# A hybrid attention trunk on one core: the linear attention's products start four projection tiles earlier, and the next norm waits for them as a chain

## The chip, the cores and the metric

The kernel runs on one NeuronCore of a Trainium2 chip. The core has a matrix engine (TensorE, in the profile PE, with its weight loads shown as PEld), three engines for elementwise work (VectorE or DVE, ScalarE or ACT, GpSimd or POOL) and a queue that mostly issues transfers (SyncE or SP). Each engine works off its own queue in order and waits for the others through semaphores. The metric is the device time of one execution in microseconds (us).

## What is computed

One layer of a streaming encoder, on 2048 tokens of width 1024, in float32. One input projection feeds three groups of heads, which all read the same normalised input; the groups are gated, concatenated, and mapped back by one output projection.

```python
h = rmsnorm(x, norm_g)
z = h @ w_in                    # columns: aq ak av ag | mq mk mv mo mi mf mg | gq gk gv ga gg
y_a = band_chunk_attention(aq, ak, av, rel_bias) * silu(ag)
qk  = silu(causal_conv([mq, mk], conv_w))
y_b = sigmoid(mo) * head_rmsnorm(mlstm_chunkwise(qk, mv, mi, mf)) * silu(mg)
log_alpha = log_sigmoid(ga @ w_alpha + b_alpha) / 16
y_c = head_rmsnorm(gla_chunkwise(gq, gk, gv, log_alpha)) * silu(gg)
out = rmsnorm(x + [y_a, y_b, y_c] @ w_out, final_g)
```

The linear attention (GLA) is the part that moves here. Inside a chunk it needs, for every pair of a query and an earlier key, a product over the channels with a decay of its own for each channel. The kernel forms the nearest pairs (within 16 tokens) one distance at a time.

## The kernel before

The first phase goes through four blocks (NQ = 4) of 512 tokens (QT). For each block it runs the projections as tiles of 24 matmuls of 512 columns (three for each of 8 k-tiles, since each operand is split in a high and a low part). A tile is cut in two pieces of 12 matmuls. In program order a block has:

- proj_z (2 tiles: GLA's queries and keys), proj_v (4 tiles for the mLSTM's values, then proj_gg with 2 tiles for GLA's gate, then 4 tiles for the attention's values);
- proj_m (6 tiles, with the convolution on DVE), proj_gm (6 tiles, the mLSTM's gates), proj_a (9 tiles, the attention's queries, keys and gate; in the last block 5, the others follow in the second phase).

The smaller work runs beside the projections as generators, called chains:

- **prep** normalises the next block's x. prep_x (called before proj_m) loads x and takes the mean square; prep itself multiplies a ones matrix by the diagonal of the scales (L299), loads xT (4 DMAs on SP), scales it with eight DVE operations (L308) and projects the gates' inputs (L315). split_x then splits the result in high and low parts (L329, L330).
- **gates** prepares the gates of the mLSTM and of GLA: L337 and L344 on PE, a chain of ACT and DVE operations, four transposes (L379) and six small products (L388); it leaves `ls`, `rt` and `iwl`.
- **gla_in** handles two halves of 256 tokens. For each of 16 distances POOL forms a product (L652) and updates the decayed keys (L649); after each four distances PE sums them over the channels (L658). Each half has four such groups.
- **gla** follows it in four pieces, two per half: PE transposes and scores (L688 to L692), DVE assembles them (L699, L702), PE takes output and state (L709 to L716), and after a norm the output is transposed (L739) and gated (L741).
- **mlstm** goes through four chunks: L531 and a DVE/ACT decay (L534, L536); L541 with L545; L559 to L576; then DVE and POOL normalise (L585 to L601) and PE transposes the result (L610).

PE's order is written by hand in program order, and a small planner named Flow decides where a chain's next step is put. Its clock advances by 12 x 0.227 us at each piece of a projection. A chain yields (PE time, gap): its next step is due when the clock has passed the gap, and it is issued at the first piece after that. `flow.need(name)` issues the due steps of all chains, without any projection between them, until the named chain has ended. The other engines' order comes from a scheduler that takes ready instructions by priority; weight splits and PSUM evacuations have a high priority.

The PSUM bank `pw` exists once. prep, gates and gla_in all use it, and gla_in holds it through a whole half. That is why the old code calls `flow.need("gla_in")` before it starts prep. The names and lines above are those of the kernel before.

The second phase (from about 972 us) holds the banded attention and the output projection; the change does not touch it.

Of the kernel before, what the change touches and what calls it, by code (L numbers as in the profile page):

```python
# [22 lines left out]
NC = QT // L  # L23
# [81 lines left out]
def trunk_kernel(ctx: ExitStack, tc: tile.TileContext, xT, x, w_f, w_t, w_o, w_gates, norm_g, conv_w,  # L105
# [3 lines left out]
    NQ = S // QT  # L109
# [23 lines left out]
    flow = Flow()  # L133
# [8 lines left out]
    with ExitStack() as pa_:  # L142
# [151 lines left out]

        def prep(q, R, dg):
            t0 = q * QT
            yield 0.0, 0.0
            rb = bank("pw")
            nc.tensor.matmul(rb, ones, dg.rearrange("p a t -> p (a t)"), start=True, stop=True)  # L299
            rbs = g_tile([P, QT])  # L300
            nc.scalar.copy(rbs, rb)
            raws = []
            for g in range(4):
                raw = xraws.tile([P, 2, QT], FP32, name="xraw")
                nc.sync.dma_start(raw, xT[:, 2 * g:2 * g + 2, t0:t0 + QT])
                for j in range(2):
                    k = 2 * g + j
                    nc.vector.scalar_tensor_tensor(raw[:, j, :], raw[:, j, :], ng[:, k:k + 1], rbs, op0=ALU.mult, op1=ALU.mult)  # L308
                raws.append(raw)
            yield 0.9, 8.0  # L310
            gp = bank("pw")
            for g in range(4):
                for j in range(2):
                    k = 2 * g + j
                    nc.tensor.matmul(gp[32 * (k % 4):32 * (k % 4) + 32, :], wg[:, k, :], raws[g][:, j, :],  # L315
                                     start=(k < 4), stop=(k >= 4), skip_group_check=True)
                if g % 2 == 1:
                    yield 2.0, 2.0
            g1 = g_tile([P, QT])
            nc.scalar.activation(g1, gp, AF.Identity, bias=onerow)  # L320
            R["raws"], R["g1"] = raws, g1
# [121 lines left out]
        def proj_gg(X):  # L443
            gg = big.tile([P, 2, QT], FP32, name="gg", bufs=1)
            for b in range(2):
                ps = proj_f(f"gg{b}", X)
                th = silu_tile(ps)
                nc.gpsimd.tensor_scalar(gg[:, b, :], th, glg[:, b:b + 1], None, op0=ALU.mult)
            return gg
# [70 lines left out]
        def mlstm(q, qk, vs, R):  # L520
            rt, iwl = R["rt"], R["iwl"]
            for c in range(NC):
# [78 lines left out]
                nc.vector.tensor_tensor(hb.rearrange("p a b d -> p b a d"), ov[:, :, :, 0:64],  # L601
                                        sm[:, 3].unsqueeze(3).broadcast_to([P, 2, 3, 64]), op=ALU.mult)
                hf = hb.rearrange("p a b d -> p (a b d)")
                yield 1.7, 9.0
                while "gm" not in R:
                    yield 0.0, 1.0
                gm = R["gm"]
# [10 lines left out]

        b16 = lambda t: t.rearrange("p (b i) -> p b i", i=16)

        def gla_in(q, z, ls_all, G):
            NB = ST // 16
            for sub in range(2):
                ts_ = slice(sub * ST, (sub + 1) * ST)
                qq, k, ls = z[:, 0, ts_], z[:, 1, ts_], ls_all[:, ts_]
                al = one.tile([P, ST], FP32, name="al")
                nc.scalar.activation(al, ls, AF.Exp, scale=1.0 / 16)
                gk = one.tile([P, ST], FP32, name="gk")
                nc.gpsimd.tensor_copy(gk, k)
                lc = big.tile([P, ST], FP32, name="lc")  # L630
                nc.vector.tensor_tensor_scan(lc, rst16, ls, 0.0, op0=ALU.mult, op1=ALU.add)
                qt = big.tile([P, ST], FP32, name="qt")
                nc.scalar.activation(qt, lc, AF.Exp, scale=1.0 / 16)
                dl = big.tile([P, 2, 8], FP32, name="dl")
                nc.vector.tensor_copy(dl, qt.rearrange("p (c b i) -> p c b i", c=2, i=16)[:, :, :, 15])
                nc.vector.tensor_tensor(b16(lc), b16(lc)[:, :, 15:16].broadcast_to([P, NB, 16]), b16(lc), op=ALU.subtract)
                nc.scalar.activation(lc, lc, AF.Exp, scale=1.0 / 16)
                nc.vector.tensor_tensor(lc, lc, k, op=ALU.mult)
                nc.vector.tensor_tensor(qt, qq, qt, op=ALU.mult)
                Dt = big.tile([P, 2, 9, 9], FP32, name="Dt")  # L640
                nc.gpsimd.memset(Dt, 1.0)
                for i in range(1, 9):
                    nc.vector.tensor_tensor(Dt[:, :, i, 0:i], Dt[:, :, i - 1, 0:i],
                                            dl[:, :, i - 1:i].broadcast_to([P, 2, i]), op=ALU.mult)
                dr_ps = bank("pw")
                yield 0.0, 4.0
                for c in range(16):
                    if c:
                        nc.gpsimd.tensor_tensor(b16(gk)[:, :, 0:c], b16(gk)[:, :, 0:c],  # L649
                                                b16(al)[:, :, c:c + 1].broadcast_to([P, NB, c]), op=ALU.mult)  # L650
                    pc = b16(prd[:, c % NP, :])
                    nc.gpsimd.tensor_tensor(pc[:, :, 0:c + 1], b16(gk)[:, :, 0:c + 1],  # L652
                                            b16(qq)[:, :, c:c + 1].broadcast_to([P, NB, c + 1]), op=ALU.mult)
                    if c % NP == NP - 1:
                        yield 0.0, 6.0
                        for e in range(c - NP + 1, c + 1):
                            w = 16 if e < 4 else e + 1
                            nc.tensor.matmul(b16(dr_ps[32 * (e % 4):32 * (e % 4) + 32, 0:ST])[:, :, 0:w], hs4[:, e // 4, :],  # L658
                                             b16(prd[:, e % NP, :])[:, :, 0:w], start=(e < 4), stop=(e >= 12), skip_group_check=True)
                        yield 0.35, 0.0  # L660
                dr = n_tile([P, ST], "dr")
                nc.scalar.copy(dr, dr_ps[:, 0:ST])
                G[sub] = (lc, qt, Dt, dr)
# [83 lines left out]
        R = {}  # L747
# [3 lines left out]
        X = split_x(R["raws"])  # L751
        flow.start("gates", gates(0, R["g1"], R))
        for q in range(NQ):
            st["q"] = q
            flow.need("gla_in")
            flow.need("gla")
            z = proj_z(X)
            vs, vg, gg = proj_v(X, lambda: proj_gg(X))
            flow.need("gates")
            G = {}  # L760
            flow.start("gla_in", gla_in(q, z, R["ls"], G))
            flow.start("gla", gla(q, vg, gg, G))
            flow.need("mlstm")
            if q + 1 < NQ:
                dg = prep_x(q + 1)
            qk = proj_m(X)
            M = dict(R)
            flow.start("mlstm", mlstm(q, qk, vs, M))
            M["gm"] = proj_gm(X)
            if q + 1 < NQ:  # L770
                flow.need("gla_in")
                R = {}
                flow.start("prep", prep(q + 1, R, dg))
            proj_a(q, X)
            if q + 1 < NQ:
                flow.need("prep")
                X = split_x(R["raws"])
                flow.start("gates", gates(q + 1, R["g1"], R))
# [332 lines left out]
```

## Time and profile before

| | us |
|---|---|
| median of 3 runs | 1402.09 |
| lowest and highest run | 1397.63, 1406.93 |
| the profiled execution | 1396.99 |
| its span, first to last instruction | 1395.3 |
| its mean granted TensorE clock | 0.958 |

A profile is of one execution. "Busy" is the time in which an engine ran instructions; matmuls overlap, so a busy PE need not run at its peak. The granted clock is the share of full speed that TensorE got. In a view of windows each line is a stretch of time with the busy time of each engine in it. In a view of waits each line says which instruction stood idle and which one ended its wait. In a timeline each line has its start and its duration, then the engine, the kernel's line, the operation and the tiles.

### The profile page before, as it was taken

To read this page: it belongs to the slowest core of one execution; us is meant where nothing else is said; L and a number is where in the kernel's file an instruction comes from. 1 tells how busy PE (TensorE), PEld (TensorE's weight loads), DVE (VectorE), ACT (ScalarE), POOL (GpSimd) and SP (SyncE) were. 2 spreads that over 40 slices of the span, in tenths; PEclk is the share of its full clock that TensorE was granted. 3 is DMA by queue.
4 is the path that set the end of the run, shared out by engine and by line. 5 is a ranking of instruction groups with operands and counts; after the bars stand their busy time and mean duration, and the time that the engine had idled before them with its cause. 6 is when DMAs were issued, how large, how long until landed. Compare 5 with 4: busy or idle time off the path is not lost.

```text
span 1395.3 us, 20018 instructions
## 1 busy us (share of the span) xinstructions
PE 1308.3 (94%) x7044; PEld 1060.7 (76%) x7044; DVE 809.1 (58%) x1886; ACT 602.4 (43%) x1149; POOL 609.2 (44%) x847
## 2 busy tenths in 40 slices
PE   4999999999998999999899999997968999999997
PEld 2787778788777878877688787886857877877876
DVE  7626566562856556474556547555657756756731
ACT  5634322563432365343135434221566645645631
POOL 4225752431665234277322526631354453453452
PEclk7999999999998999999899999996969999999999
DMA  7444224534322463422233542231596654554222
GB/s 247 141 134 135 76 71 140 190 114 136 106 77 66 135 236 90 142 87 81 75 106 117 144 151 91 82 110 49 164 274 182 183 157 149 164 170 153 78 76 84
DMA packets 107205, 180.10 MB, mean 129 GB/s; under 512 B 9824, under 2 KB 54752, under 8 KB 107104
## 3 DMA queue, kind: packets, MB, share of 16 engines
q1 hardware_dynamic: 102496, 170.43, 40.2%
q10 hardware_dynamic: 4608, 8.39, 1.6%
q8 instruction: 56, 0.92, 0.3%
q14 instruction: 45, 0.37, 0.1%
HBM read 143.14 MB, written 35.65 MB: 128 GB/s over the span
## 4 chain that ended last, share of the span: by engine, by line
PE 72%; DVE 11%; DMA 5%; ACT 4%; POOL 3%; issue 3%; SPq 1%; POOLq 0%; DVEq 0%; ACTq 0%
PE ip L243 12%; PE ip L245 11%; PE ip L244 11%; PE ip L263 3%; PE ip L265 3%; PE ip L264 3%; PE s L860 3%; PE ip L984 3%; PE ip L982 3%; PE ip L983 3%; PE tp L924 2%; DVE pt L874 2%; PE ga L692 2%; PE w L941 2%; DMA wraw<-in_w_o 2%
## 5 line engine op out<-in xcount | busy, mean ns | idle before, releaser
L243 PE MATMUL ip<-x,w 128*128 128x512 f32 x800 | 329.5, 412 | 0.0
L245 PE MATMUL ip<-x,w 128*128 128x512 f32 x800 | 314.4, 393 | 0.0
L244 PE MATMUL ip<-x,w 128*128 128x512 f32 x800 | 313.8, 392 | 0.0
L243 PEld LDWEIGHTS ip<-x,w 128*128 128x128 f32 x800 | 151.3, 189 | 45.6 <-issue 15.9
L245 PEld LDWEIGHTS ip<-x,w 128*128 128x128 f32 x800 | 151.3, 189 | 33.9
L244 PEld LDWEIGHTS ip<-x,w 128*128 128x128 f32 x800 | 151.8, 190 | 30.0 <-issue 2.6
L236 POOL TENSOR_TENSOR w<-wraw,w 128x1024 fp32r<-128x1024 f32 x44 | 106.2, 2413 | 149.1 <-ACT w L235 149.1
L235 ACT CAST w<-wraw 128x1024 fp32r<-128x1024 f32 x132 | 138.1, 1047 | 60.5 <-DMA wraw<-in_w_t 25.3
L236 DVE TENSOR_TENSOR w<-wraw,w 128x1024 fp32r<-128x1024 f32 x88 | 119.5, 1358 | 76.4 <-ACT w L235 74.9
L879 POOL TENSOR_SCALAR pt<-pt,sm 128x640 f32<-128x640 f32 (+2 forms) x96 | 70.5, 736 | 147.9 <-DVE sm L878 116.9
L982 PE MATMUL ip<-wo,y 128*128 128x512 f32 x256 | 106.7, 417 | 0.0
L263 PE MATMUL ip<-w,x 128*128 128x512 f32 x256 | 100.4, 392 | 3.6 <-ACT vg L426 3.5
L877 ACT ACTIVATE pt<-pt,sm 128x640 f32<-128x640 f32 (+2 forms) x96 | 73.3, 763 | 69.8 <-DVE sm L874 67.4
L984 PE MATMUL ip<-wo,y 128*128 128x512 f32 x256 | 101.4, 396 | 0.3 <-POOL y L890 0.3
L983 PE MATMUL ip<-wo,y 128*128 128x512 f32 x256 | 101.2, 395 | 0.0
L265 PE MATMUL ip<-w,x 128*128 128x512 f32 x256 | 99.7, 389 | 0.0
L264 PE MATMUL ip<-w,x 128*128 128x512 f32 x256 | 99.6, 389 | 0.0
L930 DVE TENSOR_TENSOR pl<-tp,ph 128x512 fp32r<-128x512 f32 (+2 forms) x126 | 74.6, 599 | 32.0 <-ACT ph L929 30.7
L860 PE MATMUL s<-kk,qq 128*128 128x384 f32 (+1 forms) x360 | 80.9, 334 | 12.4 <-DVE sm L874 10.7
L652 POOL TENSOR_TENSOR prd<-gk,zg 128x16 f32<-128x16 f32 (+15 forms) x128 | 72.2, 564 | 31.1 <-PE pw L658 24.5
L860 PEld LDWEIGHTS s<-kk,qq 128*128 128x128 f32 x360 | 60.6, 201 | 31.3 <-DVE sm L874 25.0
L929 ACT CAST ph<-tp 128x512 fp32r<-128x512 f32 (+2 forms) x126 | 63.0, 509 | 34.1 <-PE tp L924 33.3
(244 smaller groups left out, 2413.9 us busy)
## 6 DMA issues: line engine op xcount, KB each, us to landing
wraw<-in_w_f SPq DMA_DIRECT2D x100, 512.0 KB, 3.6
wraw<-in_w_t SPq DMA_DIRECT2D x32, 512.0 KB, 3.7
qq<-q_d SPq DMA_DIRECT2D x48, 256.0 KB, 4.3
kk<-k_d SPq DMA_DIRECT2D x18, 512.0 KB, 6.3
vv<-v_d SPq DMA_DIRECT2D x18, 512.0 KB, 7.1
xraw<-in_x SPq DMA_DIRECT2D x16, 512.0 KB, 5.0
xraw<-in_xT SPq DMA_DIRECT2D x16, 512.0 KB, 6.4
xr<-in_x SPq DMA_DIRECT2D x16, 512.0 KB, 3.7
```

What stands on the lines that cost most here:

```text
L235: nc.scalar.copy(w[:, :, 0, :], rv)
L236: other().tensor_tensor(w[:, :, 1, :], rv, f32(w[:, :, 0, :]), op=ALU.subtract)
L243: nc.tensor.matmul(ps, w[:, k, 0, :], X[k][:, 0, :], start=(k == 0), stop=False)
L244: nc.tensor.matmul(ps, w[:, k, 0, :], X[k][:, 1, :], start=False, stop=False)
L245: nc.tensor.matmul(ps, w[:, k, 1, :], X[k][:, 0, :], start=False, stop=(k == KT - 1))
L263: nc.tensor.matmul(ps, X[k][:, 0, t], w[:, 0, :], start=(k == 0), stop=False)
L264: nc.tensor.matmul(ps, X[k][:, 0, t], w[:, 1, :], start=False, stop=False)
L265: nc.tensor.matmul(ps, X[k][:, 1, t], w[:, 0, :], start=False, stop=(k == KT - 1))
L860: nc.tensor.matmul(sp[:, :cn], qq[:, l, tt * P:(tt + 1) * P], kk[:, ko + c0:ko + c0 + cn], start=(l == 0), stop=(l == 1))
L982: nc.tensor.matmul(ps, Y[k][:, 0, t], wo[k, j][:, 0, :], start=(e == 0), stop=False)
L983: nc.tensor.matmul(ps, Y[k][:, 0, t], wo[k, j][:, 1, :], start=False, stop=False)
L984: nc.tensor.matmul(ps, Y[k][:, 1, t], wo[k, j][:, 0, :], start=False, stop=(e == KT - 1))
```

## The change

gla_in is started inside proj_v, after proj_gg and before the four tiles of the attention's values; it was started after them. It now takes the gates' results from the dictionary R and waits, as a chain, until `iwl` is there. The wait for the gates moves from the end of proj_v to the end of proj_m. `flow.need("gla_in")` before prep is gone: prep, as a chain, yields until gla_in has ended. In all blocks but the last, the mLSTM's last chunk has its final transpose due 17 us after the step before it, where it was 9.

```diff
         def prep(q, R, dg):
             t0 = q * QT
-            yield 0.0, 0.0
+            while "gla_in" in flow.chains:
+                yield 0.0, 1.0
             rb = bank("pw")
...
                 hf = hb.rearrange("p a b d -> p (a b d)")
-                yield 1.7, 9.0
+                yield 1.7, 9.0 if c < NC - 1 or q == NQ - 1 else 17.0
                 while "gm" not in R:
...
-        def gla_in(q, z, ls_all, G):
+        def gla_in(q, z, R, G):
             NB = ST // 16
+            while "iwl" not in R:
+                yield 0.0, 1.0
+            ls_all = R["ls"]
             for sub in range(2):
...
             z = proj_z(X)
-            vs, vg, gg = proj_v(X, lambda: proj_gg(X))
-            flow.need("gates")
             G = {}
-            flow.start("gla_in", gla_in(q, z, R["ls"], G))
+
+            def between():
+                g = proj_gg(X)
+                flow.start("gla_in", gla_in(q, z, R, G))
+                return g
+
+            vs, vg, gg = proj_v(X, between)
             flow.start("gla", gla(q, vg, gg, G))
             flow.need("mlstm")
             if q + 1 < NQ:
                 dg = prep_x(q + 1)
             qk = proj_m(X)
+            flow.need("gates")
             M = dict(R)
             flow.start("mlstm", mlstm(q, qk, vs, M))
             M["gm"] = proj_gm(X)
             if q + 1 < NQ:
-                flow.need("gla_in")
                 R = {}
                 flow.start("prep", prep(q + 1, R, dg))
             proj_a(q, X)
```

## The prediction

> **What bounds the kernel now.** I read the page first. TensorE (PE) is busy 94% of the span and carries 72% of the chain that ended last; in the 40 slices (35 us each) its granted clock dips at the start, to 8 tenths in slices 13 and 20, and to 6 in slices 28 and 30.
>
> ```profile
> PE 1308.3 (94%) x7044; PEld 1060.7 (76%) x7044; DVE 809.1 (58%) x1886; ACT 602.4 (43%) x1149; POOL 609.2 (44%) x847
> PEclk7999999999998999999899999996969999999999
> PE 72%; DVE 11%; DMA 5%; ACT 4%; POOL 3%; issue 3%; SPq 1%; POOLq 0%; DVEq 0%; ACTq 0%
> ```
>
> So time is saved only where PE stands or runs slowly. The change touches the first phase alone (four blocks of 512 tokens, until about 972 us), so I cut windows there: a clean stretch of projections, a clean stretch of mixed work (212.10), the three places where the planner empties the product chain before the next norm (179.92, 417.95, 654.53, the last with its aftermath at 671.01), two turns from one block to the next (270.46, 510.15), and the tail of the phase. Columns: window, its length, busy us of PE, weight loads, DVE, ACT, POOL, then PE's granted clock.
>
> ```profile
> 103.56:119.98 16.42, 16.42 (x74) 13.34 (x72) 9.06 (x10) 7.86 (x12) 5.97 (x5) 1.00 0.58 181
> 179.92:194.09 14.17, 11.45 (x86) 8.85 (x85) 9.56 (x25) 4.21 (x9) 12.82 (x25) 0.76 0.26 75
> 212.10:228.00 15.90, 15.90 (x127) 12.24 (x125) 9.87 (x26) 4.90 (x10) 4.04 (x9) 1.00 0.47 154
> 270.46:277.01 6.55, 4.40 (x19) 2.86 (x18) 2.50 (x4) 3.63 (x8) 4.38 (x4) 1.00 0.88 341
> 417.95:433.78 15.83, 11.93 (x85) 8.71 (x84) 8.79 (x22) 4.21 (x9) 13.47 (x24) 0.68 0.19 54
> 510.15:515.56 5.41, 4.19 (x19) 2.94 (x18) 2.63 (x4) 3.58 (x9) 2.14 (x3) 1.00 0.98 385
> 654.53:671.01 16.48, 11.78 (x86) 8.92 (x85) 9.97 (x26) 4.21 (x9) 13.46 (x25) 0.79 0.20 53
> 671.01:696.06 25.05, 21.36 (x99) 16.91 (x98) 14.54 (x27) 4.45 (x7) 4.89 (x6) 0.86 0.26 85
> 937.16:971.74 34.58, 24.74 (x165) 22.52 (x163) 21.01 (x67) 5.70 (x13) 8.12 (x19) 0.71 0.14 36
> ```
>
> The first window holds 72 projection matmuls: 16.42/6 = 2.74 us for a piece of 12, the planner's unit. In the three barrier windows POOL is busy 81 to 90% and PE's clock is 0.68 to 0.79: PE has no projections to run and follows POOL's products. PE's waits over the whole phase (total, times, longest) say the same:
>
> ```profile
> PE mt L610 <- DVE m L601: 11.7, 4, 5.1
> PE gb L688 <- DVE n L741: 6.9, 4, 1.8
> PE pw L658 <- POOL prd L652: 6.2, 5, 1.8
> PE pw L344 <- ACT g L341: 1.6, 2, 1.2
> PE s L541 <- DVE qk L470: 1.3, 1, 1.3
> ```
>
> All 6.2 us on POOL's products lie in the barrier windows (1.0, 2.2, 3.0), as do three of the four waits on L741; of L610's waits 3.7 us lie in the aftermath at 691, 1.7 at the turn at 275, the rest in the tail.
>
> **What the barrier costs.** The same steps run at full clock elsewhere. Start to next start, in the clean mixed stretch and beside it:
>
> ```profile
> 169.64 0.64 PE L658 MATMUL pw<-prd,hs 128*32 128x256 f32 x8
> 170.21 0.50 PE L243 MATMUL ip<-x,w 128*128 128x512 f32 x1
> ...
> 208.99 0.49 PE L610 MATMUL mt<-ident,m 128*128 128x128 f32 x3
> 209.24 0.48 PE L243 MATMUL ip<-x,w 128*128 128x512 f32 x1
> ...
> 212.10 0.27 PE L688 MATMUL gb<-ident,dr 128*128 128x128 f32 x1
> 213.80 0.87 PE L531 MATMUL s<-hl_nm,sel 128*128 128x128 f32 x6
> 214.60 1.07 PE L315 MATMUL pw<-xraw,wg 128*32 128x512 f32 x8
> 218.54 0.94 PE L541 MATMUL s<-qk 64*128 64x128 f32 x12
> 219.88 1.07 PE L315 MATMUL pw<-xraw,wg 128*32 128x512 f32 x8
> 223.73 0.59 PE L709 MATMUL ga<-Sbd,q 128*128 128x256 f32 x2
> 225.34 0.94 PE L559 MATMUL s<-Cbd,qk 128*128 128x130 f32 x6
> 228.00 0.50 PE L243 MATMUL ip<-x,w 128*128 128x512 f32 x1
> ```
>
> L688 to L692 1.70, L531 0.80, L541 with L545 1.34, L709 to L716 1.61, L559 to L576 2.66, L610 0.25, L658 at most 0.57, L739 (two transposes) about 0.2. A barrier holds one each of the first four, an L610, an L739 and three L658: 7.6 us. Lost: 14.17 - 7.6 = 6.6, then 8.2, then 8.9. The aftermath of the third holds five pieces (13.7), L559 to L576, an L299 (estimate 0.5, at most half the 1.0 of the eight L315), an L739 and an L610: 17.3 us, so 7.8 more are lost. **Sum 31.5 us.** Blocks 0 and 1 show no such aftermath.
>
> **The change part by part.** *Where the chain now runs.* The planner's order on PE follows from the yields and a piece of 12 x 0.227 us, so I walk it; the walk of the old code gives the old trace's PE order step for step. Old: gla_in starts after 12 tiles, 22 us later than after 8 (four tiles of two pieces). In its old place its eight PE groups stand 10 to 12 us apart, two are left when proj_gm ends, and the barrier issues them bare. New: it opens before the second proj_t; the gates have long ended there (their last step falls in proj_gg both ways), so the new wait for iwl, and the moved wait for the gates, cost nothing; that cover is one proj_gg tile, 5.5 us, and every us beyond it would be PE's. Six groups are out by the middle of proj_gm, the seventh falls in proj_gm, the eighth one piece into proj_a, and prep's first matmul follows one piece later. POOL needs 16 x 0.564 for the products (row below) and about as much for the keys per half, some 18 us, against 50 planned, so it keeps pace, and in the 103.56 window it is busy only 5.97 of 16.42 us. On POOL gla_in passes proj_v's share of the weight splits, which run ahead by priority anyway; its DVE and ACT set-up needs only z and the gates and was early before. It issues no DMA, and no instruction is added. prep keeps its 4 loads of xT on SP's queue, which pass proj_a's weight loads as before, and its 8 L308 on DVE. Barrier loss 31.5 us goes: low 15.0 (its idle alone), high 31.5. I take 31.5, because the moved steps then lie between projections as in the 212.10 window, at clock 1.00.
>
> *The turn of the block.* Old, at the turn, PE waits for the last mLSTM chunk's L610 and then the gates' L344: a piece, L610 and L344 (0.5, from 276.45 to 277.01 here) would fill 3.5 us, so 6.55 - 3.5 = 3.1 and 5.41 - 3.5 = 1.9, **5.0 us**. The third turn shows none. With a due time of 17 for the last L610 it falls five pieces into proj_v; it holds one bank (mt) nobody else wants before the next chunk. L344 is now planned 8 us after L337 instead of 4. I take all 5.0 back (low 0).
>
> *What comes in their place.* Without the barrier the mLSTM chain stands four to six pieces later against the projections, and prep's DVE work lands beside other steps:
>
> ```profile
> L652 POOL TENSOR_TENSOR prd<-gk,zg 128x16 f32<-128x16 f32 (+15 forms) x128 | 72.2, 564 | 31.1 <-PE pw L658 24.5
> L308 DVE SCALAR_TENSOR_TENSOR xraw<-xraw,ng,g 128x512 f32<-128x512 f32 x32 | 27.5, 921 | 3.4 <-ACT g L301 3.4
> L236 DVE TENSOR_TENSOR w<-wraw,w 128x1024 fp32r<-128x1024 f32 x88 | 119.5, 1358 | 76.4 <-ACT w L235 74.9 <-DMA xraw<-in_xT 1.2
> L534 DVE SCALAR_TENSOR_TENSOR dd<-s,rt,cap 128x128 f32<-128x128 f32 x96 | 26.6, 344 | 7.7 <-PE s L531 7.6
> L699 DVE TENSOR_TENSOR at<-gb,msk 128x128 f32<-128x128 f32 x64 | 14.1, 281 | 4.0 <-ACT kdt L695 3.9
> L702 DVE TENSOR_TENSOR at<-ga,at 128x448 f32<-128x448 f32 x16 | 10.0, 624 | 5.4 <-PE ga L692 5.1
> 276.45 1.13 PE L344 MATMUL pw<-g,gsel 128*128 128x512 f32 x2 [0.42 <-ACT g L341]
> 298.64 0.16 DVE L375 TENSOR_TENSOR hl_iw<-rows,hl_iw 6x4 fp32r<-6x4 f32 x1
> 302.35 0.60 PE L379 MATMUL pw<-ident,rows 128*128 128x128 f32 x4
> 956.83 1.52 PE L531 MATMUL s<-hl_nm,sel 128*128 128x128 f32 x6
> 971.74 0.78 PE L243 MATMUL ip<-x,w 128*128 128x512 f32 x1
> ```
>
> (a) prep's eight L308, 8 x 0.921 = 7.4 us on DVE, now precede the third gla piece's L699 and L702 (4 x 0.281 + 0.624 = 1.7) and L711 comes 11 us after L299. With two weight splits (L236, 2.7) DVE has about 12 us of work in front of L711, and PE queues everything behind it. Low 0 (cover enough), high 7.4 a block; I take 2.5, **7.5 us** for three blocks. (b) At the turn the last chunk's six L534 (2.1 us) meet the split of x: low 0, high 2.5; I take 0.5, **1.5**. (c) Its later DVE work, about 5 us (six state updates and the normaliser), now lies beside the gates. The gates' rows were ready 3.7 us before L379 and the new order leaves them 2.4 less. Low 0, high 5 - 1.3 = 3.7; much of it fits while DVE waits for ACT's log-sigmoid; I take 0.5, **1.5**. (d) gla's first L699 and L702 now come before the last conv output that L541 waits for (1.3 once before), and L541 comes 1.6 us later: low 0, high 1.3 + 1.7 = 3.0; I take 0.5 in four blocks, **2.0**. (e) Tail: fewer steps are left (two L688 to L692, an L610, an L709 to L716, an L739, 5.5 us of work, have moved ahead and are paid there), but two mLSTM chunks in a row remain at 14.9 us each (956.83 to 971.74) and 1 us of gla: 30.8 after 34.6. So 5.5 - 3.8 = **1.7** more (low -2, high 5.5).
>
> **The sum.** 31.5 + 5.0 - 7.5 - 1.5 - 1.5 - 2.0 - 1.7 = 22.3 us off. The profiled execution took 1396.99 us (span 1395.3): 1374.7. The median of the runs shown is 1402.09, 5.1 above it; by it 1379.8. I take **1377**, between them.
>
> **A rule that speaks against it.** All idle in the barriers and the aftermath together is 6.2 + 3 x 1.7 + 3.7 = 15.0 us; the other 16.5 us of my 31.5 is slow running at clocks of 0.68 to 0.86. The Trainium skill, page "TensorE: Matmul & The Clock Gate", Part 1, says that the clock halves only after an idle window of about 3.4 us; by it no gap in the first two barriers is long enough, and the lower clock would not be owed to the waiting. The trace does not agree: the longest gap in the first three barrier windows is 1.8 us and the clock fell in all of them.
>
> **Rivals.** *The clock loss stays* (0.07). If small chain matmuls lower the clock wherever they stand, only 15.0 us and the turns' 5.0 come back, against 14.2 of new waits: 5.8 off, **1391**. Against it: window 212.10 holds the same steps at 1.00. *The norm's block on DVE takes its full price* (0.13): (a) at 7.4 a block, 22.2 instead of 7.5: 7.6 off, **1389**. For it: the 3.7 us wait of L610 at 691 is just such a block, L308 ahead of L601; against it: in blocks 0 and 1 the same block cost PE nothing. *No new wait at all* (0.20): 36.5 off, **1360**. *Slower* (0.07): the last chunk crossing the turn delays the whole gates chain, which PE then awaits bare at L379 with proj_v's second half behind it. It decides against the change from 36.5/3 = 12.2 us a turn; at 17 us, most of the 22.2 from L344 (276.45) to L375, the time is 1397 - 36.5 + 51 = **1411**. For it: chunk and gates share DVE's queue; against it: rows cover only the 3.7 us of (c) and the 2.5 of (b). That the chain doesn't start earlier in truth, because POOL was already ahead, is no rival of its own: PE's order, not POOL's, held the old end.
>
> **Chances.** Forecast 0.53 (own range 1364 to 1388), no new wait 0.20, the two small gains 0.20, slower 0.07. The range 1359 to 1394 reaches from the full gain to the small ones. About 1% is what a measurement of this kernel can tell from no change, so 14 us: faster 0.70 (the full gain and most of the forecast), same 0.23, slower 0.07.
>
> **What would show it.** Right: no stretch of over one L658 without projections before proj_a, the waits of L658 on L652 gone, clock 1.00 there, and no L610 wait at the turns. (a) is right if L711 or L564 waits behind L308 by 2 to 3 us. Wrong: new PE waits at L379, L541 or L711 of over 5 us a block, or barrier steps that stay slow between projections.

## The result, and the profile after

| | before | after |
|---|---|---|
| median of 4 runs, us | 1400.95 | 1364.33 |
| lowest and highest run, us | 1397.63, 1406.93 | 1360.25, 1367.73 |
| the profiled execution, us | 1396.99 | 1360.25 |
| its span, us | 1395.3 | 1358.5 |
| its mean granted clock | 0.958 | 0.972 |

The ratio is 0.9751 (95% interval 0.9725 to 0.9777): 36.6 us by the medians, 36.7 by the two profiled executions. The prediction said 1377 and a range of 1359 to 1394.

In the changed kernel the lines stand 1 to 8 lower: L610 and L601 have become L611 and L602, L344 L345, L308 L309, L379 L380, L541 L542, L652 and L658 L656 and L662, L699, L702, L709 and L711 L703, L706, L713 and L715. Below, each fence has its own kernel's numbers, the text after it names the same line as its fence, and experiments with an edit of their own are shifted by some lines more.

The page of the changed kernel, the parts shown of before:

```profile
PE 1289.8 (95%) x7044; PEld 1045.6 (77%) x7044; DVE 815.6 (60%) x1886; ACT 600.7 (44%) x1149; POOL 628.4 (46%) x847
...
PEclk7999999999999999999999999997959999989999
...
PE 76%; DVE 10%; DMA 5%; ACT 4%; issue 3%; POOL 2%; SPq 0%; POOLq 0%; DVEq 0%; ACTq 0%
```

The number of instructions is the same on each engine. PE's busy time fell by 18.5 us, because the same matmuls ran at a higher clock; the dips to 8 tenths in slices 13 and 20 are gone, and between the start and the second phase the only dip left is the tail (slice 28, 7 tenths).

Where the time went shows in marks that both traces have: the start of each block's gates product (L344 before, L345 after), the last mLSTM transpose, which ends the first phase, and the end of the span. In us from the start:

| | before | after | saved in this stretch |
|---|---|---|---|
| block 0's gates product | 41.5 | 41.8 | -0.3 |
| to that of block 1 | 234.9 | 227.9 | 7.0 |
| to that of block 2 | 238.6 | 229.8 | 8.8 |
| to that of block 3 | 242.9 | 227.6 | 15.3 |
| to the end of the first phase | 213.8 | 211.3 | 2.5 |
| second phase | 423.6 | 420.2 | 3.4 |

The mark has moved a little in PE's order: from block 1 on one more piece of a projection and one L610 less stand ahead of it after the change, 2.5 us of work (2.74 - 0.25). For equal work the first stretch therefore saved 9.5 us and the last one of the first phase nothing.

The windows of the changed kernel, in the columns of the prediction: around prep's DVE block in block 0, a turn of the block, and the tail.

```profile
188.00:213.90 25.90, 25.90 (x176) 19.77 (x175) 20.25 (x49) 8.19 (x16) 9.70 (x13) 1.00 0.40 123
273.42:294.20 20.78, 19.82 (x88) 15.84 (x87) 18.65 (x55) 16.54 (x32) 8.47 (x22) 1.00 0.12 41
910.32:938.37 28.05, 15.63 (x109) 13.90 (x108) 15.68 (x48) 3.71 (x6) 5.22 (x11) 0.76 0.12 31
```

There is nothing left that corresponds to the three barrier windows: prep now begins among projections, and PE is busy in the first of these windows from end to end at a clock of 1.00, where the barrier had 0.76. PE's waits until 950 us (total, times, longest), without the start of the program:

```profile
PE mt L611 <- DVE m L602: 11.4, 3, 5.8
...
PE ip L263 <- ACT vg L427: 4.2, 4, 1.8
PE s L542 <- DVE dd L535: 1.4, 2, 0.7
...
PE ga L713 <- DVE at L706: 0.4, 1, 0.4
PE pw L662 <- POOL prd L656: 0.4, 1, 0.4
```

The 6.2 us on POOL's products are down to 0.4, and the four waits on L741 have gone. Two of L611's three waits (5.8 and 5.1) lie in the tail, the third is 0.4; none is at a turn. Ahead of the tail no new wait of more than 1.8 us has come. In the tail the first of the two was 1.2 before: less other work is left there to lie over it.

### The profile page after: what moved, and what is told of

It reads as the page before. It is cut to its first block, busy times and chain, and to the rows that moved or that the text cites. A ratio compares the mean times of both kernels' runs of the same rounds, so it can differ in the third digit from the quotient of the medians.

```text
span 1358.5 us, 19994 instructions
## 1 busy us (share of the span) xinstructions
PE 1289.8 (95%) x7044; PEld 1045.6 (77%) x7044; DVE 815.6 (60%) x1886; ACT 600.7 (44%) x1149; POOL 628.4 (46%) x847
## 4 chain that ended last, share of the span: by engine, by line
PE 76%; DVE 10%; DMA 5%; ACT 4%; issue 3%; POOL 2%; SPq 0%; POOLq 0%; DVEq 0%; ACTq 0%
PE ip L243 13%; PE ip L245 12%; PE ip L244 12%; PE ip L263 3%; PE ip L265 3%; PE ip L264 3%; PE ip L992 3%; PE ip L990 3%; PE ip L991 3%; PE s L868 3%; PE tp L932 2%; DVE pt L882 2%; PE ga L696 2%; PE w L949 2%; PE s L565 1%
## 5 line engine op out<-in xcount | busy, mean ns | idle before, releaser
L236 DVE TENSOR_TENSOR w<-wraw,w 128x1024 fp32r<-128x1024 f32 x88 | 123.2, 1400 | 81.3 <-ACT w L235 80.8
L263 PE MATMUL ip<-w,x 128*128 128x512 f32 x256 | 101.3, 396 | 4.2 <-ACT vg L427 4.2
L656 POOL TENSOR_TENSOR prd<-gk,zg 128x16 f32<-128x16 f32 (+15 forms) x128 | 73.8, 576 | 64.0 <-PE pw L662 57.8
L398 ACT ACTIVATE e<-ip 128x512 f32<-128x512 f32 x44 | 26.2, 594 | 126.5 <-PE ip L245 108.1
```

What stands on the lines that cost most here:

```text
L236: other().tensor_tensor(w[:, :, 1, :], rv, f32(w[:, :, 0, :]), op=ALU.subtract)
L263: nc.tensor.matmul(ps, X[k][:, 0, t], w[:, 0, :], start=(k == 0), stop=False)
```

## The experiments

The theory after the result: the barrier was worth its full 31.5 us, and the new order's collisions on DVE were covered, though by little. The rivals: that one part of the change alone brings the time, and that the barrier's length was the slow clock's doing. Each part was undone alone, two were done alone, and the disputed costs were then raised.

**The barrier put back.** The early start and the due time of 17 stay.

```diff
         def prep(q, R, dg):
             t0 = q * QT
-            while "gla_in" in flow.chains:
-                yield 0.0, 1.0
+            yield 0.0, 0.0
...
             if q + 1 < NQ:
+                flow.need("gla_in")
                 R = {}
```

> The changed kernel with the old barrier put back: prep no longer waits as a chain, and all due steps are issued bare until the product chain has ended. The early start and the due time of 17 stay. Theory A (the early start alone empties the barrier): by the planner's walk only the eighth L658 group is left for the barrier in each block, against three groups and ten other steps before; POOL has had that group ready, so the time is that of the changed kernel, 1364, within 4 us, and no window at the old barrier place shows a clock under 0.95. Theory B (the barrier itself costs, because it forces the other chains): at least 5 us a block come back, so 1379 or more.

1377.36, ratio 0.9849 (0.9824 to 0.9875). The windows of this kernel: the three places of the barrier, then the turn into block 3.

```profile
184.86:186.46 1.60, 1.47 (x12) 0.43 (x10) 1.10 (x2) 1.40 (x2) 1.00 (x3) 1.00 0.38 38
416.99:417.87 0.88, 0.88 (x12) 0.30 (x10) 0.47 (x2) 0.68 (x2) 0.00 (x0) 1.00 0.80 326
650.61:651.49 0.88, 0.88 (x12) 0.30 (x10) 0.47 (x2) 0.68 (x2) 0.00 (x0) 1.00 0.73 298
733.20:780.34 47.14, 42.86 (x203) 34.53 (x202) 29.61 (x73) 23.16 (x40) 22.77 (x36) 0.96 0.48 122
```

The early start empties the barrier by itself: 14 to 16 us have become 0.9 to 1.6, at full clock. Yet the kernel is 13 us slower than the changed one. The stretches from gates product to gates product are 228.0, 230.9, 233.8, 219.4, so blocks 0 and 1 lose 0.1 and 1.1 and blocks 2 and 3 lose 6.2 and 8.1 (by equal work 2.7, 1.1, 6.2 and 5.5, since the last chunk's L564 step, 2.6 us, stands behind the mark here). PE's waits in the last window say what is late there:

```profile
PE mt L610 <- DVE m L601: 1.9, 1, 1.9
PE ip L263 <- ACT vg L426: 1.3, 1, 1.3
PE pw L388 <- DVE rt L383: 1.0, 1, 1.0
```

The short barrier issues the due mLSTM steps at another place, the last chunk stands two or three pieces later, and at the turn it runs into the gates' rows. PE stands for 2.2, 3.0 and 4.3 us in such windows of the three turns (268.50:312.06, 499.40:545.70 and the one above), where the changed kernel's have 1.0, 0 and 1.2, and the clock of 0.96 in two of them is worth 3.7 more (an estimate): together 11 of the 13 us. The windows went as the first theory had them, the time nearly as the second; neither had this reason.

**The start put back.** gla_in starts after proj_v, as before; the chain wait and the 17 stay.

```diff
                 g = proj_gg(X)
-                flow.start("gla_in", gla_in(q, z, R, G))
                 return g
 
             vs, vg, gg = proj_v(X, between)
+            flow.start("gla_in", gla_in(q, z, R, G))
```

> The changed kernel with the product chain opened at its old place, after the attention's value tiles; prep still waits as a chain. Theory A (early start is the half that matters): the last groups now lie under proj_a and cost nothing there, but gla ends later than the block, and by the walk its last output step, the mLSTM's L541 and L564 and the gates' L337 and L344 are issued bare at each of the three turns, so a new barrier appears there: 5 to 9 us a turn, 1380 to 1392 in all. Theory B (taking out the barrier is enough): within 5 us of 1364.

1388.0, ratio 0.9949 (0.9928 to 0.9971). A window at the turn of block 0, and the PE timeline inside it:

```profile
256.93:271.40 14.47, 11.03 (x70) 8.42 (x69) 8.08 (x20) 12.86 (x22) 6.28 (x5) 0.73 0.92 316
```

```profile
264.45 1.22 PE L345 MATMUL pw<-g,gsel 128*128 128x512 f32 x1 [3.44 <-ACT g L342]
```

As expected by the first theory: the bare stretch has not gone but moved, to the turn, where gla's remaining steps are issued without projections, and a new wait of the gates on ACT stands in it (three, 8.9 us in all). So the barrier's loss is recovered only with products that start earlier; without it, waiting as a chain pushes the same work into the next place that has to be empty.

**The due time put back.** All chunks have 9 again.

```diff
-                yield 1.7, 9.0 if c < NC - 1 or q == NQ - 1 else 17.0
+                yield 1.7, 9.0
```

> The changed kernel with the last chunk's L610 due after 9 us again. By the walk it then stands after two pieces of proj_v instead of five. Theory A (the later due time is needed): in the changed kernel's trace L610's input is ready 16 to 18 us after L564 at the first turn, and the shorter place gives PE 8 us less: 3 to 7 us of waiting at each of three turns, 1373 to 1385. Theory B (DVE's order follows PE's place and the input comes earlier too): within 3 us of 1364.

1385.81, ratio 0.9918 (0.9897 to 0.994), a median 21.5 us above the changed kernel's. The last chunk's transpose waits at each turn, 7.1, 5.4 and 5.1 us, and in the window of the first of these waits the clock is 0.87. The waits are those the first theory expected, the time lies just above its range.

**The due time alone**, on the kernel before:

```diff
-                yield 1.7, 9.0
+                yield 1.7, 9.0 if c < NC - 1 or q == NQ - 1 else 17.0
```

> The kernel before with one edit: the last chunk's L610 due after 17 us instead of 9. By the walk it stands two pieces later, after proj_z's third piece and the gates' L344. Theory A (in the old order the last chunk's L564 lies ahead of the block's turn and its input for L610 is some 6 us late at most): only the 5.0 us lost at two turns can come back, so 3 to 6 us off the kernel before (ratio 0.996 to 0.998). Theory B (the due time is worth as much here as in the changed kernel, where 9 costs 22 us): 12 us or more off. Theory C (no effect in the old order): ratio 1.000.

1394.59, ratio 0.9969 (0.9955 to 0.9983): 4.3 us, against the 5.0 that the prediction read from the two turns. In its profile the stretches to blocks 1 and 2 are, for equal work, 2.7 and 1.4 us shorter, where the prediction had 3.1 and 1.9.

**The early start alone**, on the kernel before, so with barrier and 9:

```diff
+            while "iwl" not in R:
+                yield 0.0, 1.0
...
-            vs, vg, gg = proj_v(X, lambda: proj_gg(X))
...
+                flow.start("gla_in", gla_in(q, z, R, G))
...
+            vs, vg, gg = proj_v(X, between)
```

> The kernel before with the early start alone: the barrier before prep and the due time of 9 are as before. Theory A (the early start is what pays and the other edits trim it): 1377 to 1386, 13 us or more off the kernel before. Theory B (without the later due time the last chunk's L610 waits at the turn as long as in the run with 9 us, and with the barrier back the tail is longer too): 1390 to 1400, hardly better than before.

1398.12, ratio 0.9999 (0.9986 to 1.0011): nothing, where the barrier is as empty as in the first experiment. Its PE waits tell why:

```profile
PE mt L610 <- DVE m L601: 37.4, 5, 10.2
```

37.4 us in five waits, against 11.7 in four before; three of the five, 8.1, 8.1 and 10.2 us, stand at the turns, so all that the barrier gave is paid there. So the parts don't add:

| early start | chain instead of barrier | due 17 | us against before |
|---|---|---|---|
| yes | no | no | 0 |
| no | no | yes | -4 |
| no | yes | yes | -7 |
| yes | yes | no | -11 |
| yes | no | yes | -21 |
| yes | yes | yes | -35 |

(Each ratio less 1, times 1400.) The 17 is worth 4 us in the old order and some 23 in the new one, 21.5 by the medians. The chain in place of the barrier was not run alone.

**What the transpose waits for at the turn.** In the kernel with 9, the timeline of DVE and POOL ahead of the 7.1 us wait, and the wait:

```profile
280.63 0.57 POOL L600 TENSOR_TENSOR sm<-sm 128x6 f32<-128x6 f32 x1
...
280.41 1.38 DVE L635 TENSOR_TENSOR_SCAN lc<-rst,ls 128x256 f32<-128x256 f32 x2
281.83 1.28 DVE L350 TENSOR_TENSOR_SCAN g<-g,ml 6x512 f32<-6x512 f32 x1
283.04 1.40 DVE L354 TENSOR_TENSOR_SCAN g<-ones,g 6x128 f32<-6x128 f32 x4
284.47 0.97 DVE L292 TENSOR_SCALAR g<-ident,rs 128x128 f32<-128x128 f32 x4
285.37 1.21 DVE L236 TENSOR_TENSOR w<-wraw,w 128x1024 fp32r<-128x1024 f32 x1
...
287.32 0.56 DVE L602 TENSOR_TENSOR m<-m,sm 128x384 f32<-128x384 f32 x1
...
287.94 0.90 PE L611 MATMUL mt<-ident,m 128*128 128x128 f32 x3 [7.10 <-DVE m L602]
```

POOL hands over the last scale at 281.2, and DVE multiplies (L602) at 287.3, six us later: in between it works through the scans of the products and the gates, the next norm's diagonal and a weight split, in the order that the scheduler gave it. One variant of this kernel gives the last chunk's work from its output to that multiplication a higher priority, to move it ahead of the others:

```diff
+                with tc.high_priority(offset=AHEAD) if c == NC - 1 and q < NQ - 1 else ExitStack():
...
```

> The changed kernel with the last chunk's L610 due after 9 us again, as in the run that cost 22 us, and the last chunk's work from L564's results to the normalised tile given the high priority that weight splits have. Theory A (the wait of 5 to 7 us at each turn is DVE's order: in that run the tile's last DVE operation stood 6 us behind the gates' operations after its input was ready): the waits of L610 at the turns fall to 2 us or less and the time to 1364 to 1372. Theory B (the latency of the chunk's own DVE and POOL chain is too long for 9 us wherever it stands in the queues): the waits stay over 4 us and the time over 1380.

1389.34, ratio 0.9932 (0.9903 to 0.996). The priority changed nothing: in the two traces DVE, ACT and POOL work off the same instructions in the same order from end to end, so that this is a second run of the kernel with 9. Its input is ready at 282.55 and the multiplication runs at 288.67, again six us later, and PE waits 7.85 us. What another order on DVE would give is therefore not shown. The other variant takes work off the turn. ACT's squares of the next x are scaled by a 1.0 that is computed from the gates' `iwl`, so they can't run before the gates have ended:

```diff
+                nc.vector.tensor_scalar(sc, after, 0.0, 1.0, op0=ALU.mult, op1=ALU.add)
...
-                nc.scalar.activation(xt, xt, AF.Square, accum_out=rs[:, tt:tt + 1])
+                nc.scalar.activation(xt, xt, AF.Square, scale=sc, accum_out=rs[:, tt:tt + 1])
```

> The changed kernel with the last chunk's L610 due after 9 us again, and the next x's squares (8 ACT operations, with the accumulator reads, some 5 us and their loads' waits) kept from the turn: each is scaled by a 1.0 that is worked out from the gates' last result, so that they run after it. In the run with 9 us and in the one with the higher priority, DVE stood idle for 6 to 7 us at the turn behind a weight split whose ACT half came after these squares, and the last chunk began late. Theory A (the squares in ACT's queue make the last chunk late): L610's waits at the turns fall from 5 to 7 us to 2 or less, and the time from 1386 to 1364 to 1372. Theory B (the gates' own operations on DVE and the small POOL steps make it late): the waits stay over 4 us and the time over 1380.

1376.8, ratio 0.9856 (0.9827 to 0.9884), 9 us better than without the edit. Not all of that is the turns': of the 12.1 us between the two profiles 5.7 lie in the second phase, where nothing was edited.

```profile
275.25 0.57 POOL L604 TENSOR_TENSOR sm<-sm 128x6 f32<-128x6 f32 x1
281.04 0.56 DVE L606 TENSOR_TENSOR m<-m,sm 128x384 f32<-128x384 f32 x1
281.65 0.68 PE L615 MATMUL mt<-ident,m 128*128 128x128 f32 x3 [4.43 <-DVE m L606]
```

Counted from the gates' product (at 267.89 here, at 271.51 without the edit), the input came 1.8 us earlier and the multiplication 2.7, and a distance of five us between them stayed; waits of 4.4, 4.4 and 5.1 us remain, after 7.1, 5.4 and 5.1. Neither theory alone: the squares account for 3.6 us of the three waits, and for the rest PE waits for DVE's place for L606. With the 17 the need for it moves behind that place: in the changed kernel L602 stands at the same place of DVE's order and runs at 285.89, and L611 runs at 287.10, without a wait (timeline below). Why the scheduler puts that multiplication behind the gates' work was not found.

**What made the barrier long.** On the kernel before, PE gets something to do in it: after each step that the barrier issues, two matmuls whose result nothing reads.

```diff
-                flow.need("gla_in")
+                wf = bank("ip", 2)
+                while "gla_in" in flow.chains:
...
+                    flow.step(n)
+                    for _ in range(2):
+                        nc.tensor.matmul(wf, X[0][:, 0, 0:P], X[0][:, 0, :], start=True, stop=True)
```

> The kernel before with the barrier kept and two extra projection-sized matmuls, with no reader, after each step issued inside it, so that PE's clock stays up while POOL's products are awaited; the output is not touched. Theory A (the barrier's length is POOL's: 12.8 to 13.5 us of POOL work in 14 to 16.5 us): the clock in the three barriers rises to 0.9 or more and the barriers keep their length within 1.5 us each; the time is that of the kernel before, within 5 us (1396 to 1406). Theory B (16.5 of the 31.5 us are slow running, as the prediction had it): the barriers shorten by 3 to 5 us each and the third's aftermath by 3, so 1386 to 1392.

1394.5, ratio 0.9974 (0.9957 to 0.9991). Its windows, the three barriers and the stretch after the third:

```profile
180.34:195.94 15.60, 13.86 (x108) 9.92 (x107) 10.12 (x26) 4.59 (x10) 13.72 (x25) 1.00 0.23 70
418.39:435.06 16.67, 14.21 (x107) 10.06 (x107) 8.18 (x24) 4.58 (x10) 14.82 (x26) 1.00 0.18 52
655.71:671.88 16.17, 14.79 (x108) 10.60 (x108) 9.59 (x25) 4.58 (x10) 13.36 (x25) 0.89 0.18 54
671.88:694.86 22.98, 19.31 (x99) 15.51 (x98) 14.94 (x28) 4.07 (x6) 4.89 (x6) 0.93 0.27 84
```

The clock in the barriers rose from 0.76, 0.68 and 0.79 to 1.00, 1.00 and 0.89, and they are hardly shorter or even longer: 15.60, 16.67 and 16.17 us after 14.17, 15.83 and 16.48. POOL is busy 83 to 89% of them, as it was 81 to 90% before. So in the main POOL's work sets the length of a barrier. The filler is itself about 5.0 us of PE work in each (22 matmuls of 0.227), so the run doesn't show that a full clock alone would gain nothing; but with POOL's work as it was, a faster PE could at best have taken off the 1.4, 2.4 and 3.0 us in which POOL stood. The time lies between those that the theories gave: 2.1 us of the 3.8 between the two profiles were gained in the stretch after the third barrier (22.98 after 25.05), 1.8 in the second phase, which has no filler.

**How much cover is left ahead of L713.** The changed kernel, with one more DVE operation of the size of L309 that changes no value, once behind each of prep's four loads of xT, or behind every second one:

```diff
+                nc.vector.scalar_tensor_tensor(raw[:, 1, :], raw[:, 1, :], 0.0, raw[:, 1, :], op0=ALU.mult, op1=ALU.add)
```

> The changed kernel with four more DVE operations of 128x512 in prep, each multiplying half of a loaded tile by 0 and adding the tile itself, so that the result is the same: the norm's block on DVE grows from 8 to 12 operations, by about 3.0 us a block. In the changed kernel's trace L706 ends 0.6 us before L711 starts. Theory A (the block's cover is nearly used up): L711 waits about 2.4 us in each of three blocks, 7 us more, 1370 to 1373. Theory B (the scheduler moves gla's operations ahead of the longer block, or the wait is made up before the next step that DVE holds): within 3 us of the changed kernel.

> The changed kernel with two more DVE operations of 128x512 in prep instead of four, some 1.5 us a block, the result the same. With four, 3.0 us more on DVE cost 5.3 to 7.2 us in each of three blocks and 4.7 us before the first block, because PE waited 3.3 us for L707 and then ran at a clock of 0.70 for 11 us. Theory A (the loss is the wait, and the wait of 1.5 us is too short for the clock to fall): about 1.5 us in each of three blocks and 2.3 before the first, 7 us in all, 1369 to 1371. Theory B (in proportion to four): half of 20.7, 1373. Theory C (the cover of 0.6 us swallows much of it): 4 us or less, under 1367.

The four cost 1383.16, ratio 0.9895 (0.9876 to 0.9914); the two 1372.31, ratio 0.982 (0.9797 to 0.9842). First the waits and a window of the kernel with four, then the PE timeline and two windows of that with two.

```profile
PE ga L714 <- DVE at L707: 8.3, 4, 3.3
```

```profile
211.84:223.25 11.41, 11.41 (x69) 8.57 (x69) 5.75 (x20) 0.91 (x2) 2.94 (x5) 0.70 0.21 83
```

```profile
210.03 0.76 PE L715 MATMUL ga<-Sbd,q 128*128 128x256 f32 x1 [2.67 <-DVE at L708]
444.76 0.45 PE L715 MATMUL ga<-Sbd,q 128*128 128x256 f32 x1 [1.10 <-DVE at L708]
```

```profile
210.03:222.99 12.96, 12.96 (x68) 9.81 (x69) 5.82 (x20) 0.91 (x2) 2.42 (x5) 0.61 0.22 76
430.00:455.00 25.00, 23.90 (x159) 18.34 (x158) 20.91 (x51) 8.78 (x16) 8.18 (x14) 1.00 0.35 111
```

The wait that term (a) of the prediction described comes as soon as DVE has a few operations more, so the cover is real but thin. (Of the 8.3 us, 0.45 are a wait in the third block that the changed kernel has too.) The price was the surprise: with four operations, 2.6 to 3.5 us more on DVE a block, PE waited 3.26, 2.30 and 2.33 us, but the blocks were 5.6, 5.3 and 7.1 us longer, because PE ran at 0.70, 0.70 and 0.55 for the 11 us after each wait. With two operations, block 0 has a wait of 2.67 us and is 8.7 longer (7.4 against the second profile of the changed kernel below), at 0.61 for the 13 us that follow; blocks 1 and 2 have waits of 1.1 at a clock of 1.00 and are 0.9 and 1.1 longer. Block 0's wait is the longer one because one of its two operations took 2.23 us, where the others take 0.67 to 0.86: it met a weight split on POOL.

```profile
206.44 2.37 POOL L236 TENSOR_TENSOR w<-wraw,w 128x1024 fp32r<-128x1024 f32 x1 [2.24 <-ACT w L235]
207.12 2.23 DVE L311 SCALAR_TENSOR_TENSOR xraw<-xraw 128x512 f32<-128x512 f32 x1
```

The time with two lies between those that the theories gave.

**A shorter tail.** The last block's first-chunk transpose waits as deferred work until proj_gm has its gate, so that the second chunk can begin.

```diff
...
+                pend.append((hf, cs))
+                if q < NQ - 1 or c == NC - 1 or len(pend) > 1:
+                    while "gm" not in R:
+                        yield 0.0, 1.0
+                while pend and "gm" in R:
...
```

> The changed kernel with the mLSTM's first chunk of the last block not held up for the gates' tile: its final transpose L610 is put off until the gates are there, and the second chunk begins meanwhile. By the walk two chunks' first halves move under projections and the tail after the last projection keeps L564 of the third chunk and the whole fourth chunk. Theory A (the tail is the mLSTM's serial latency, 14 us a chunk): the tail falls from 28 us to about 22, less the work paid earlier, so 3 to 6 us off the changed kernel, 1358 to 1361. Theory B (the second chunk moved ahead collides with the gates' and gla's DVE work under proj_gm): within 2 us of it or slower.

1359.39, ratio 0.972 (0.9702 to 0.9737), the best of all that were run. The window of its tail:

```profile
913.35:938.30 24.95, 14.14 (x88) 12.75 (x87) 12.36 (x38) 2.87 (x5) 5.20 (x11) 0.62 0.13 35
```

The tail is 3.1 us shorter than 28.05, and the first phase ends at 938.2 as in the changed kernel (938.3): the chunk's work was paid earlier. The medians are 3.0 us apart and the intervals of the two ratios just touch (the changed kernel beside it: 0.9737 to 0.9776), and the profile doesn't have the gain in the part that was edited. So it stays open whether this version is the faster one.

**The changed kernel again**, beside the ones above:

> The changed kernel once more, on the same chip as the other runs of this call, for a second profile of it: the first phase within 1 us of the first profile's 938.3 us, and the second phase, which the change does not touch, anywhere between 420 and 424 us as in the profiles so far. Theory A (the 3.4 us that the second phase was shorter in the first profile are its own spread): it comes out longer than 420.2. Theory B (the change shortened it): it stays under 421.

1362.42, ratio 0.9756 (0.9737 to 0.9776). The first phase ends at 938.8, and the second takes 420.9. It repeats the first phase within 0.5 us but doesn't settle what the second phase does, since 420.9 fits both theories. Over all runs its length lies between 418 and 425 us, with 424.0 for the kernel that has only the 17, 421.0 for the one with only the early start, though nothing in it was edited and its instructions have the same order on DVE, ACT and POOL in both profiles of before and after. How much of the 3.4 us saved there is owed to the change stays open.

## Why the prediction was right and where it was wrong

The sign, the place and the size of the gain were right; the likeliest time was 13 us too high by the medians, and by the sum 14.4 (1374.7 against the profiled 1360.25). Step by step:

**The barrier and the turns** were priced at 6.6 and 3.1 us for block 0, 8.2 and 1.9 for block 1, and 16.7 (with the aftermath) for block 2: 36.5. For equal work the three stretches lost 9.5, 8.8 and 15.3, so 33.6 of the 36.5 came back there, and the price of each single block was right within 1.4 us. The 2.9 between them is all that came in place, where the terms (a) to (d) had 12.0 for these blocks. The turns show it: the window at 273.42 holds seven pieces (19.2) and a transpose (0.25) in 20.78 us, so 1.4 more than its work, 0.96 of it a wait of L263 for ACT. The same work from L345 on takes 39.28, 37.89 and 39.38 us at the three turns, so the third loses as much and the second nothing.

**The split of the barrier's loss** into 15.0 of idle and 16.5 of slow running was wrong in its meaning. Of the 16.5, 12.4 lie in the barriers themselves (23.7 less 11.3 of idle). With the clock at 1.00, 1.00 and 0.89 these were not shorter to speak of, so most of the 12.4 was no loss of the clock: PE kept step with POOL, which was busy 81 to 90% there. In the aftermath (the other 4.1) the clock did cost something. The sum was not harmed, since the whole barrier goes, but the low bound of 15.0 and the rival "the clock loss stays" lost their ground.

**Where the chain now runs**: PE's order in the new trace is as the prediction has it. In each of the first three blocks the eighth product group stands one piece into proj_a and prep's first matmul one piece later, and the last chunk's transpose five pieces into proj_v. But the walk says only when PE is asked. What DVE does in the meantime was not walked, and on it the terms below rest. The rows of DVE, ACT and PE in the changed kernel's timeline:

```profile
195.70 5.59 DVE L309 SCALAR_TENSOR_TENSOR xraw<-xraw,ng,g 128x512 f32<-128x512 f32 x8
201.59 0.87 DVE L703 TENSOR_TENSOR at<-gb,msk 128x128 f32<-128x128 f32 x4
203.85 0.61 DVE L706 TENSOR_TENSOR at<-ga,at 128x448 f32<-128x448 f32 x1
...
204.60 0.67 PE L713 MATMUL ga<-Sbd,q 128*128 128x256 f32 x2
...
285.89 0.56 DVE L602 TENSOR_TENSOR m<-m,sm 128x384 f32<-128x384 f32 x1
...
287.10 0.49 PE L611 MATMUL mt<-ident,m 128*128 128x128 f32 x3
...
291.93 0.63 ACT L370 ACTIVATE rows<-rows 6x512 f32<-6x512 f32 x1
...
294.20 0.60 PE L380 MATMUL pw<-ident,rows 128*128 128x128 f32 x4
```

**Term (a)**, 7.5 us predicted, came to 0: no L713 waits behind prep's block (the one wait of 0.4 is at 603 us, before it). The block of eight operations ran in 5.6 us in the first two blocks and in 6.75 in the third, not in 7.4:

```profile
L309 DVE SCALAR_TENSOR_TENSOR xraw<-xraw,ng,g 128x512 f32<-128x512 f32 x8 | 5.6, 768 | 0.0
```

The prediction took the mean of all 32 (921 ns), but the trace of before has the right price:

```profile
L308 DVE SCALAR_TENSOR_TENSOR xraw<-xraw,ng,g x32: 737/746/2712, 21.0 to 689.7; 128x512 f32<-128x512 f32 x32
```

28 of the 32 took 737 to 751 ns and start some 0.66 us apart; the other four took 1.7 to 2.7 us, each beside a split on POOL, and three of them belong to the start of the program. Nor did the two weight splits (2.7 us) stand in the queue here: from L309's start to L706's end DVE needs 8.8 us in the first two blocks and 9.9 in the third, not 12. In the three blocks L706 ends at 204.46, 433.62 and 661.83 and L713 starts at 204.60, 433.76 and 661.98: the ends met within 0.2 us, so the low end (0) held, by luck as far as the prediction goes, and the two added-work experiments show how near a wait was.

**Terms (b) and (c)**, 1.5 each, came to 0. The prediction read the gates' cover from L375, which writes hl_iw; the transposes L379 read rows, which ACT finished at 297.80, 4.5 us ahead of L379. After the change ACT's L370 ends at 292.56 and L380 starts at 294.20: 1.6 us are left there, and more at the two later turns. But the prediction priced the crossing of chunk and gates at 3.7 a turn at most, and without the 17 it is 5.1 to 7.1 of waiting and over 20 us in the time. The step that failed is the one that booked the due time as 5.0 us from the turns of the old trace: its larger part is to keep the transpose behind DVE's place for L602. The margin at the first turn is 0.65 us (285.89 + 0.56 to 287.10). The rival "slower" had the right place, not the right engine order: the transpose waits for the gates, not the gates for the chunk.

**Term (d)**, 2.0, came to 0: no wait on the convolution's last output, where before had one of 1.3.

**Term (e)**, 1.7 more, came to about 0: the tail went from 34.58 to 28.05, 6.5 us, for 5.5 of work moved ahead, so 1.0 less, but for equal work the last stretch as a whole saved nothing.

**What nothing had foreseen**: 3.4 us in the second phase, which the change doesn't touch. So of the 14.4 us, 11.0 are new waits and the tail, priced at 14.2 and come to 3.2 (2.9, and 0.3 before the first block), and 3.4 the second phase. The rival "no new wait at all" (1360) came nearest; the forecast's mechanism was the same, with terms set above the low end of their bounds where the low end held. That the rival's 36.5 comes within 0.2 of the measured 36.7 is luck: the 3.4 of the second phase happen to fill the 3.2 that new waits took.

## What to carry to other kernels

Before an emptied stretch is priced, look at which engine is busy in it: here POOL at 81 to 90% said that the slow PE was mostly a follower, and filling PE bore it out. Before a mean is used as a price, look at the single rows: four slow operations made 746 ns into 921. Where two long chains cross on one in-order engine, walk that engine's order too, not only the matrix engine's: a due time that looks like a detail (4 us alone) can be what holds a move together (over 20 us). Undo each part by itself, and do each by itself: two parts of this change gave 0 and 4 us alone, and the three 35 together.

## What was not expected of the hardware

The granted clock answered to short waits, by more than their own length. The kernel with two added operations around its wait of 2.67 us, and the first barrier of the kernel before:

```profile
206.56:209.97 3.41, 0.81 (x4) 0.34 (x2) 3.41 (x6) 0.00 (x0) 2.25 (x1) 1.00 0.07 10
209.97:220.21 10.24, 10.18 (x57) 7.84 (x58) 4.91 (x17) 0.91 (x2) 1.02 (x1) 0.50 0.29 101
...
180.37:183.78 3.41, 1.70 (x15) 1.46 (x15) 3.10 (x9) 1.93 (x3) 3.14 (x6) 1.00 0.04 17
183.78:190.60 6.82, 6.82 (x40) 5.65 (x39) 4.27 (x12) 1.56 (x6) 6.43 (x15) 0.50 0.47 126
```

The clock is 1.00 or 0.50 in these windows, and it stays low for 3.41 us or a whole multiple: 10.24 after the wait of 2.67, and 6.82, 6.82 and 10.24 after the waits of 3.26, 2.30 and 2.33 with four operations. A wait then costs its own length and half the low stretch, 2.67 + 5.1 = 7.8 us for the block that was 7.4 to 8.7 longer (an estimate). After waits of 1.1 us it stayed at 1.00. In each of the three barriers of the kernel before, the fall followed a single wait of 1.7 us (L688), but the length of a wait alone doesn't decide: after L610's wait of 1.73 at the first turn the clock stayed at 1.00. With filler beside the same steps those waits were 0.8 to 1.4 us and the clock 0.89 to 1.00. The Trainium skill, page "TensorE: Matmul & The Clock Gate", Part 1, puts the idle window after which the clock falls at about 3.4 us. The low stretches here agree with that length, but PE need not be idle throughout: it was busy for 0.81 and 1.70 us of the 3.41 before the two falls shown. How densely PE must work to keep its clock these runs don't show.
